# Two transformer blocks on one core: attention values with V as the weight, staged gelu, and two pieces of work in another order

## The chip, the core and the metric
One core of a Trainium2 chip. The kernel is one launch; its time is device microseconds, the median of the runs shown. All data are f32 in memory.

## What is computed
The reference runs two transformer blocks on x (512 tokens, width 1024), batch 1.

Block 1: RMS norm; a projection to q, k, v of 8 heads of 64, to gelu inputs u and vg (512 columns each) and a forget gate per head; causal attention with a cumulated log-forget bias; beside it a spatial gate over chunks of 128 tokens, u times (w_s applied to the normalised gelu(vg), plus a bias); `h = x + concat(att, sg) @ w_out`; an FFN of width 2816 with a causal depthwise convolution of 3 taps; a final RMS norm.

Block 2: an adaptive norm whose shift, scale and gates come from `silu(c) @ w_ada`; 8 heads of chunk attention ("ca", head size 64, normalised q and k, relative bias) and 8 heads of latent attention ("mla", 96 columns for q and k, rope on 32, 64 for v); an output projection, and an FFN of the same form.

```
p = softmax(logits)             # per head and 128 queries
out = einsum('bhqk,bkhd->bqhd', p, v)
uv = gelu(proj[..., V_END:G_END])
return rmsnorm(h, norm_final_g) # end of block 1
```

## The kernel before
Wide matrix products run as three float32r products each (high x high, high x low, low x high), so every weight piece is split: `load_split` (L337 to L353) reads a raw piece by a transfer on SP's queue, ScalarE casts it to the high part (L350), VectorE or GpSimd subtracts to get the low part (L351). `prefetch` keeps two pieces ahead (LOOK). There are 4 high and 4 low buffers.

TensorE's order is the program's own, written by hand; the other engines' order is made by a scheduler from the program's order and priorities. `high_priority` pulls work ahead, a negative offset pushes it behind, and `late()` (L528) orders an instruction behind the last one marked `urgent`. Two lists of generators, `Fill` objects, feed the attention loop: `fill` holds products (each yields its estimated ns), `bg` holds elementwise background work. `run(ns)` takes steps until the ns are used up, `upto(name)` takes all steps up to the end of a named job.

`attention` (L619 to L676) walks strips of 128 queries of one head. In step t it issues the scores of strip t (`strip_scores`, two or three products, a bias add with a running minimum on VectorE at L597, exp on ScalarE at L601), background work, half of the step's fill, the transposes of the exponentials of strip t-1 (`strip_turn`, L610, and their copy to pt at L612), the other half of the fill, and the values of strip t-2 (`strip_values`, L617): for each block of 128 keys a plain f32 product with P^T as the weight and 64 columns of V streaming, accumulated in the one `o` bank. Every 8 strips, that is two heads, `pair_end` (L709) takes the reciprocals of the 8 sums, scales `o` into `att` (L717), and one step later `turn` transposes att four times (L725) and splits the result into a high and a low part of `mix` (L741, L742). The last two heads run in half pairs of 4 strips. PSUM in attention has 4 `mm` banks, 3 `s` banks and 1 `o` bank. The p tiles, the gelu's and the norm's temporaries share one pool of 3 buffers (`pp`).

In block 1 the gelu is `gelu2` (L1108): two GpSimd instructions, a VectorE multiply (L1114), tanh on ScalarE (L1115) and a VectorE multiply into uv (L1116), on one token tile of 128x256 at a time. `gate(j)` (L1118) adds the squares on GpSimd and their sums on VectorE, `gelu_u(j)` (L1143) does the u columns; both are background work. The evacuation of q and k of a pair is at L1182 (qf) and L1186 (kf, marked urgent).

In block 2 `start` and `cq0` (L1473, L1489) compute the first projections; then `bg` gets the norm of cq0, the rope tables and `final`, block 1's final norm of x (L932 to L945: a scalar instruction, a pow on GpSimd, eight small products on TensorE and 16 VectorE multiplies at L942 into x in place). `ca_head` (L1615) transposes normalised q and k (L1633), then stacks them with copies (L686, L687, L696, L697) and a transfer of half a tile. `fill` goes through cq1, ck1, mla0, cv1, mla1 and the output products; `out0` first takes `bg` up to `final`, as it adds to x.

Of the kernel before, what the change touches and what calls it, by code (L numbers as in the profile page):

```python
# [19 lines left out]
P = 128  # L20
# [216 lines left out]
class Kernel:  # L237
# [367 lines left out]
    def strip_turn(self, hd, qi, sp):  # L605
        nk = (qi + 1) * P
        s, p = sp
        for kb in range(qi + 1):
            c = slice(kb * P, (kb + 1) * P)
            self.nc.tensor.transpose(s[:, c], p[:, c], self.ident)  # L610
        pt = self.pt.tile([P, 512], F32, tag="pt", name="pt")
        self.nc.any.tensor_copy(out=pt[:, :nk], in_=s[:, :nk])  # L612
        return pt

    def strip_values(self, hd, qi, pt, o):
        for kb in range(qi + 1):
            self.mm(o, pt[:, kb * P:(kb + 1) * P], hd["v"](kb), kb == 0, kb == qi)  # L617

    def attention(self, heads, fill, rate, bg, bgrate, mix, depth=1):  # L619
# [21 lines left out]
        for t in range(n + depth + 3):  # L641
            r = rate(t)
            if t < n:
                h, qi = seq[t]
                slices(h)
                sc[t] = self.strip_scores(hd[h], qi)
                for h in range(len(heads)):
                    if 0 < seq.index((h, 0)) - t <= LEAD:
                        slices(h, 1)
            with self.tc.high_priority(offset=-BEHIND):  # L650
                bg.run(bgrate(t))
            fill.run(r / 2)
            u = t - depth
            if 0 <= u < n:
                h, qi = seq[u]
                pt[u] = self.strip_turn(hd[h], qi, sc.pop(u))
            if t > n + depth:
                for f in later:
                    f()
                later = []  # L660
            fill.run(r / 2)
            for f in later:
                f()
            later = []
            u -= 1
            if 0 <= u < n:
                h, qi = seq[u]
                if u % 8 == 0:
                    o = self.bank("o")
                ov = 2 * qi + h % 2  # L670
                self.strip_values(hd[h], qi, pt.pop(u), o[:, ov * 64:(ov + 1) * 64])
                if h < last:
                    if u % 8 == 7:
                        later = [self.pair_end(o, mix, *hd[h]["end"])]
                elif u % 4 == 3:
                    later = [self.pair_end(o, mix, *hd[h]["end"], half=u % 8 // 4)]  # L676
# [32 lines left out]
    def pair_end(self, o, mix, sums, at, pool, tag, half=None):  # L709
# [4 lines left out]
        c8, c512 = slice(2 * qs[0], 2 * qs[-1] + 2), slice(qs[0] * P, (qs[-1] + 1) * P)  # L714
        nc.vector.reciprocal(sums[:, c8], sums[:, c8])
        att = self.att.tile([P, 512], F32, tag="att", name="att")
        nc.vector.tensor_tensor(out=att[:, c512].rearrange("p (g d) -> p g d", d=64),  # L717
                                in0=o[:, c512].rearrange("p (g d) -> p g d", d=64),
                                in1=sums[:, c8].unsqueeze(2).to_broadcast([P, 2 * len(qs), 64]),
                                op=ALU.mult)  # L720

        def turn():
            tp = self.bank("s")
            for t in qs:
                nc.tensor.transpose(tp[:, t * P:(t + 1) * P], att[:, t * P:(t + 1) * P], self.ident)  # L725
            if not half:
                t = pool.tile([P, 2, 512], F32R, tag=tag, name="mix")
                mix[at] = t[:, 0], t[:, 1]
            ins = self.split(mix[at], tp, c512)
            if half:  # L730

                self.before = ins
            mix[at, half] = True
# [299 lines left out]
    def block1_mix(self, xn, x, evac, evac_last, norm_a):  # L1033
        nc, i = self.nc, self.i
        ctx = self.c_mix = ExitStack()
        self.pt = self.pool("pt", 3, ctx=ctx)
# [50 lines left out]
        sqs = self.pt.tile([P, 512], F32, tag="pt", name="sqs")  # L1087
# [20 lines left out]
        def gelu2(v):  # L1108

            t = self.pp.tile([P, 512], F32, tag="p", name="gelu")[:, :256]  # L1110
# [3 lines left out]
            nc.vector.tensor_tensor(out=t, in0=t, in1=v, op=ALU.mult)  # L1114
            nc.scalar.activation(out=t, in_=t, func=AF.Tanh, scale=float(np.sqrt(2 / np.pi)))  # L1115
            nc.vector.scalar_tensor_tensor(out=v, in0=t, scalar=1.0, in1=v, op0=ALU.add, op1=ALU.mult)  # L1116

        def gate(j):  # L1118

            vs = [uv[t][:, 512 + 256 * j:768 + 256 * j] for t in range(4)]  # L1120
            for t, v in enumerate(vs):
                gelu2(v)
                sq = self.pp.tile([P, 512], F32, tag="p", name="sqg")[:, :256]
                nc.gpsimd.tensor_tensor(out=sq, in0=v, in1=v, op=ALU.mult)
                nc.vector.tensor_reduce(out=ss[:, j, t], in_=sq.rearrange("p (g d) -> p g d", d=64),
                                        axis=AX.X, op=ALU.add)
                yield 1200
# [15 lines left out]
        def gelu_u(j):  # L1143
            for t in range(4):
                gelu2(uv[t][:, 256 * j:256 * j + 256])
                yield 700
# [214 lines left out]
    def block2_mix(self, xn, norm_b, final, evac, evac_last, norm_a):  # L1361
# [3 lines left out]
        self.pt = self.pool("pt2", 3, ctx=ctx)  # L1365
# [4 lines left out]
        stk = self.pool("stk2", 12, ctx=ctx)  # L1370
# [94 lines left out]
        def ca_job(w, z, j, **kw):  # L1465
# [4 lines left out]
            if z < 2 and kw.get("pairs") != ((0, 1),):  # L1470
                bg.add(w, ca_norm(z, j))

# [16 lines left out]
        def cq0():  # L1489
# [3 lines left out]
            bg.add("final", final)  # L1493
# [195 lines left out]
        heads = [ca_head(h) for h in range(8)] + [mla_head(h) for h in range(8)]  # L1689
        self.attention(  # L1690
# [36 lines left out]
```

## Time and profile before
| | us |
|---|---|
| median of 3 runs | 1229.65 (1225.97 to 1230.58) |
| profiled execution, its own time | 1225.62 |
| span of that execution | 1223.9 |

The span runs from the first to the last instruction. PE is TensorE, PEld its weight loads, DVE VectorE, ACT ScalarE, POOL GpSimd. A TensorE record is longer than the spacing of records, since consecutive products overlap in the pipeline; the cost of one in a stream is the difference of two starts. A plain f32 product leaves two records, one for each of its passes. In brackets stand the idle time ahead of an instruction and what ended it.

### The profile page before, as it was taken

To read this page: it belongs to the slowest core of one execution; us is meant where nothing else is said; L and a number is where in the kernel's file an instruction comes from. 1 tells how busy PE (TensorE), PEld (TensorE's weight loads), DVE (VectorE), ACT (ScalarE), POOL (GpSimd) and SP (SyncE) were. 2 spreads that over 40 slices of the span, in tenths; PEclk is the share of its full clock that TensorE was granted. 3 is DMA by queue.
4 is the path that set the end of the run, shared out by engine and by line. 5 is a ranking of instruction groups with operands and counts; after the bars stand their busy time and mean duration, and the time that the engine had idled before them with its cause. 6 is when DMAs were issued, how large, how long until landed. Compare 5 with 4: busy or idle time off the path is not lost.

```text
span 1223.9 us, 17406 instructions
## 1 busy us (share of the span) xinstructions
PE 1193.0 (97%) x6730; PEld 1038.9 (85%) x6730; DVE 780.2 (64%) x1392; ACT 526.5 (43%) x946; POOL 190.5 (16%) x209
## 2 busy tenths in 40 slices
PE   9999898999999999999998989999999999999998
PEld 6898688988888888888998988899988888888887
DVE  6646777688888887433575878876675665653221
ACT  6535445454444443323434556655544444442110
POOL 2367301300000000000245472301200000000000
PEclk9999999999999999999999999999999999999999
DMA  7432222166666666433121333111133323233330
GB/s 237 120 102 78 82 82 61 53 188 196 200 192 190 193 190 190 144 98 128 58 86 57 87 109 104 36 36 36 53 123 102 103 86 104 93 89 112 114 110 18
DMA packets 42594, 135.78 MB, mean 111 GB/s; under 512 B 5120, under 2 KB 6016, under 8 KB 42512
## 3 DMA queue, kind: packets, MB, share of 16 engines
q1 hardware_dynamic: 34096, 106.84, 28.3%
q10 hardware_dynamic: 8208, 27.27, 7.4%
q8 instruction: 52, 0.85, 0.3%
q0 software_dynamic: 208, 0.57, 0.2%
q14 instruction: 30, 0.25, 0.1%
HBM read 128.37 MB, written 2.10 MB: 107 GB/s over the span
## 4 chain that ended last, share of the span: by engine, by line
PE 84%; DVE 6%; POOL 4%; issue 2%; ACT 2%; DMA 1%; SPq 0%; ACTq 0%; DVEq 0%; POOLq 0%
PE mm L372 74%; PE s L372 4%; PE o L372 3%; PE s L610 2%; POOL wlo L351 1%; ACT whi L350 1%; DVE wlo L351 1%; DVE s L597 1%; DVE ca L1457 1%; DMA x<-in_xT_dram 1%; POOL gelu L1111 0%; PE mm L1667 0%; DVE nt L557 0%; ACT p L601 0%; PE s L725 0%
## 5 line engine op out<-in xcount | busy, mean ns | idle before, releaser
L351 DVE TENSOR_TENSOR wlo<-wraw,whi 128x1024 fp32r<-128x1024 f32 (+4 forms) x182 | 210.3, 1157 | 180.6 <-ACT whi L350 179.5
L372 PE MATMUL mm<-xnh,whi 128*128 128x512 f32 (+1 forms) x832 | 310.8, 374 | 5.6 <-DVE x L877 2.7
L350 ACT CAST whi<-wraw 128x1024 fp32r<-128x1024 f32 (+4 forms) x194 | 191.6, 991 | 277.8 <-PE mm L372 260.2
L372 PE MATMUL mm<-xnl,whi 128*128 128x512 f32 (+1 forms) x832 | 309.7, 372 | 0.0
L372 PE MATMUL mm<-xnh,wlo 128*128 128x512 f32 (+1 forms) x832 | 309.7, 372 | 0.0
L372 PEld LDWEIGHTS mm<-xnh,whi 128*128 128x128 f32 x832 | 156.2, 188 | 33.5 <-DVE x L877 2.9
L372 PEld LDWEIGHTS mm<-xnh,wlo 128*128 128x128 f32 x832 | 156.1, 188 | 27.6
L372 PEld LDWEIGHTS mm<-xnl,whi 128*128 128x128 f32 x832 | 156.2, 188 | 26.7
L372 PE MATMUL mm<-gh,whi 128*128 128x512 f32 (+1 forms) x384 | 141.3, 368 | 1.1 <-DVE x L967 0.6
L372 PE MATMUL mm<-gh,wlo 128*128 128x512 f32 (+1 forms) x384 | 141.1, 367 | 0.0
L372 PE MATMUL mm<-gl,whi 128*128 128x512 f32 (+1 forms) x384 | 141.0, 367 | 0.0
L759 DVE SCALAR_TENSOR_TENSOR cv<-mm,cols,cv 128x510 f32<-128x510 f32 (+1 forms) x176 | 130.3, 745 | 2.5 <-ACT cv L757 0.5
L372 PE MATMUL mm<-whi,xnh 128*128 128x256 f32 (+3 forms) x304 | 96.5, 318 | 1.1 <-ACT xnh L842 1.1
L372 PE MATMUL mm<-wlo,xnh 128*128 128x256 f32 (+3 forms) x304 | 93.6, 308 | 0.2 <-DVE wlo L351 0.2
L372 PE MATMUL mm<-whi,xnl 128*128 128x256 f32 (+3 forms) x304 | 93.6, 308 | 0.1
L372 PEld LDWEIGHTS mm<-gh,whi 128*128 128x128 f32 x384 | 72.1, 188 | 13.5 <-DVE x L967 0.8
L372 PEld LDWEIGHTS mm<-gh,wlo 128*128 128x128 f32 x384 | 72.1, 188 | 12.1
L372 PEld LDWEIGHTS mm<-gl,whi 128*128 128x128 f32 x384 | 72.1, 188 | 12.0
L601 ACT ACTIVATE p<-s,st 128x128 f32<-128x128 f32 (+1 forms) x96 | 50.7, 528 | 70.4 <-DVE st L597 64.6
L1028 DVE CUSTOM_DVE_ANT_0 wada<-wada,cs,cols 128x1024 f32<-128x1024 f32 x48 | 61.5, 1282 | 28.9 <-DMA wada<-in_w_ada_dram 28.8
L372 PE MATMUL mm<-mix,whi 128*128 128x256 f32 (+1 forms) x288 | 73.8, 344 | 2.6 <-DVE x L877 1.5
L757 ACT ACTIVATE cv<-mm,cols 128x512 f32<-128x512 f32 x88 | 67.6, 773 | 0.0
(296 smaller groups left out, 1793.2 us busy)
## 6 DMA issues: line engine op xcount, KB each, us to landing
wraw<-in_w_up_dram SPq DMA_DIRECT2D x88, 512.0 KB, 3.6
wada<-in_w_ada_dram ACTq DMA_DIRECT2D x48, 512.0 KB, 3.7
wraw<-in_w_down_dram SPq DMA_DIRECT2D x32, 512.0 KB, 3.6
wraw<-in_w_out_dram SPq DMA_DIRECT2D x16, 512.0 KB, 3.7
wraw<-in_w_down_dram SPq DMA_DIRECT2D x16, 384.0 KB, 3.2
wraw<-in_w_qk_dram SPq DMA_DIRECT2D x8, 512.0 KB, 4.2
wraw<-in_w_v_dram SPq DMA_DIRECT2D x8, 256.0 KB, 4.9
x<-in_xT_dram SPq DMA_DIRECT2D x8, 256.0 KB, 6.5
```

The costliest lines, as they stand in the source:

```text
L350: nc.scalar.copy(hi[:, :n], raw[:, :n])
L351: (nc.gpsimd if pool else nc.vector).tensor_tensor(out=lo[:, :n], in0=raw[:, :n], in1=hi[:, :n].bitcast(F32), op=ALU.subtract)
L372: self.nc.tensor.matmul(out, lhsT, rhs, start=start, stop=stop, **kw)
L597: self.urgent = nc.vector.tensor_tensor_reduce(out=s[:, cs], in0=s[:, cs], in1=b, scale=1.0, scalar=3e38 if j == 0 else st[:, j - 1:j], op ...
L601: nc.scalar.activation(out=p[:, :nk], in_=s[:, :nk], func=AF.Exp, bias=st[:, len(parts) - 1:len(parts)], scale=-1.0, accum_out=hd["sums"](qi))
L610: self.nc.tensor.transpose(s[:, c], p[:, c], self.ident)
L757: nc.scalar.activation(out=t, in_=ps, func=AF.Identity, scale=w[2], bias=self.col(cb, n))
L759: nc.vector.scalar_tensor_tensor(out=t[:, d:], in0=ps[:, :512 - d], scalar=w[2 - d], in1=t[:, d:], op0=ALU.mult, op1=ALU.add)
L1028: nc.vector.tensor_tensor_reduce(out=w, in0=w, in1=self.cs, scale=1.0, scalar=self.col("b_ada_2", n), op0=ALU.mult, op1=ALU.add, accum_out ...
L1457: nc.vector.tensor_tensor(out=v3, in0=v3, op=ALU.mult, in1=ss[:, j, z, t].unsqueeze(2).to_broadcast([P, 4, 64]))
```

## The change
- **Values.** `strip_values` goes; `pair_values` does two heads at once at the end of a pair (in half pairs for the last two heads). V (128 keys x 64) is the weight, P^T of up to 512 queries streams, head 0 writes partitions 0 to 63 of the `o` bank and head 1 partitions 64 to 127, alternating by key block. So pt holds all blocks of a head (128 x 5 x 384, 2 buffers instead of 3 of 128 x 512).
- **Reciprocals.** `o` is now transposed already, so the four transposes of `pair_end` turn the broadcast reciprocals instead: ScalarE broadcasts 8 columns to 512, TensorE transposes them, ScalarE copies them out of PSUM, VectorE multiplies `o` by them, and the split reads SBUF.
- **Order in `attention`.** The turn of a finished pair and the values stand between the first half of the fill and the transposes of the strip.
- **Gelu.** Two token tiles at a time, with a yield between stages and `late()` on the VectorE instructions.
- **Block 2.** `final` is added to `bg` behind the norm of ck1; three rounds of `fill.run(1500)` and `bg.run(800)` stand ahead of `attention`; the stack pool has 9 tiles instead of 12.

```diff
-    def strip_turn(self, hd, qi, sp):
+    def strip_turn(self, pt, qi, sp):
...
-        pt = self.pt.tile([P, 512], F32, tag="pt", name="pt")
-        self.nc.any.tensor_copy(out=pt[:, :nk], in_=s[:, :nk])
-        return pt
-
-    def strip_values(self, hd, qi, pt, o):
-        for kb in range(qi + 1):
-            self.mm(o, pt[:, kb * P:(kb + 1) * P], hd["v"](kb), kb == 0, kb == qi)
+        a, b = divmod(qi, 3)
+        self.nc.any.tensor_copy(out=pt[:, a:a + qi + 1, b * P:(b + 1) * P],
+                                in_=s[:, :nk].rearrange("p (k q) -> p k q", q=P))
+
+    def pair_values(self, hds, pts, o, half=None):
+
+        q0, q1 = (0, 4) if half is None else (2 * half, 2 * half + 2)
+        for kb in range(q1):
+            a = max(q0, kb)
+            for z, (hd, pt) in enumerate(zip(hds, pts)):
+                p = pt.rearrange("p a b -> p (a b)")[:, (3 * kb + a) * P:(3 * kb + q1) * P]
+                self.mm(o[HALF_P[z], a * P:q1 * P], hd["v"](kb), p, kb == 0, kb == q1 - 1)
...
-            if 0 <= u < n:
-                h, qi = seq[u]
-                pt[u] = self.strip_turn(hd[h], qi, sc.pop(u))
-            if t > n + depth:
-                for f in later:
-                    f()
-                later = []
-            fill.run(r / 2)
             for f in later:
                 f()
             later = []
-            u -= 1
+            u = t - depth
+            w = u - 1
+            if 0 <= w < n and w % 8 == 7 or n - 8 <= w < n and w % 4 == 3:
+                h = seq[w][0]
+                half = None if h < last else w % 8 // 4
+                if not half:
+                    o = self.bank("o")
+                self.pair_values([hd[h - 1], hd[h]], [pt[h - 1], pt[h]], o, half)
+                later = [self.pair_end(o, mix, *hd[h]["end"], half=half)]
             if 0 <= u < n:
                 h, qi = seq[u]
...
+                if qi == 0:
+                    pt[h] = self.pt.tile([P, 5, 384], F32, tag="pt", name="pt")
+                self.strip_turn(pt[h], qi, sc.pop(u))
+            fill.run(r / 2)
...
+        att = self.att.tile([P, 512], F32, tag="att", name="att")
         nc.vector.reciprocal(sums[:, c8], sums[:, c8])
...
+        nc.scalar.copy(att[:, c512].rearrange("p (g d) -> p g d", d=64),
+                       sums[:, c8].unsqueeze(2).to_broadcast([P, 2 * len(qs), 64]))
...
-            ins = self.split(mix[at], tp, c512)
+            nc.scalar.copy(att[:, c512], tp[:, c512])
+            nc.vector.tensor_tensor(out=att[:, c512], in0=o[:, c512], in1=att[:, c512], op=ALU.mult)
+            ins = self.split(mix[at], att, c512)
...
-            t = self.pp.tile([P, 512], F32, tag="p", name="gelu")[:, :256]
+            t = self.pp.tile([P, 2, 256], F32, tag="p", name="gelu")
...
+            yield 800
+            with self.late():
+                nc.vector.tensor_tensor(out=t, in0=t, in1=v, op=ALU.mult)
             nc.scalar.activation(out=t, in_=t, func=AF.Tanh, scale=float(np.sqrt(2 / np.pi)))
...
+            yield 800
+            with self.late():
+                nc.vector.scalar_tensor_tensor(out=v, in0=t, scalar=1.0, in1=v, op0=ALU.add, op1=ALU.mult)
...
+            if w == "w_ck1":
+                bg.add("final", final)
...
-            bg.add("final", final)
...
+        for _ in range(3):
+            fill.run(1500)
+            bg.run(800)
         self.attention(
```

## Rows read from the trace of the kernel before

**Rows 1.** The page, part 1: TensorE's busy time, share, instructions.
```profile
PE 1193.0 (97%) x6730; PEld 1038.9 (85%) x6730; DVE 780.2 (64%) x1392; ACT 526.5 (43%) x946; POOL 190.5 (16%) x209
```

**Rows 2.** Busy time by stretch: length, then per engine us and count, clock, DMA.
```profile
55.00:215.00 160.00, 149.83 (x898) 129.52 (x897) 106.66 (x259) 73.97 (x165) 61.99 (x59) 1.00 0.28 82
654.50:665.00 10.50, 6.89 (x41) 6.12 (x40) 7.86 (x9) 4.86 (x6) 3.45 (x2) 0.84 0.25 63
665.00:840.00 175.00, 169.53 (x1283) 159.29 (x1284) 133.33 (x325) 101.91 (x262) 56.46 (x65) 1.00 0.23 66
```

**Rows 3.** TensorE in order of time, 654 to 665 us: start, length, instruction.
```profile
654.33 0.28 PE L372 MATMUL mm<-whi,xnl 128*128 128x256 f32 x1
...
658.45 1.21 PE L1633 MATMUL mm<-ident,ca 128*128 128x128 f32 x6 [2.17 <-DVE ca L1457]
...
659.67 0.42 PE L372 MATMUL mm<-wlo,xnh 128*128 128x256 f32 x1
...
664.90 0.36 PE L372 MATMUL s<-kl,qs 128*128 128x256 f32 x1 [0.20 <-DMA kl<-kl]
```

**Rows 4.** TensorE in order of time: three gaps in the two attention stages.
```profile
128.28 0.50 PE L372 MATMUL mm<-xnh,whi 128*128 128x512 f32 x1 [2.29 <-DVE kf L1186]
...
202.50 0.66 PE L610 MATMUL s<-ident,p 128*128 128x128 f32 x4 [0.72 <-ACT p L601]
...
708.79 0.63 PE L1633 MATMUL mm<-ident,ca 128*128 128x128 f32 x4 [2.66 <-DVE qs L687]
```

**Rows 5.** VectorE in order of time, ahead of two of these gaps.
```profile
127.20 0.42 DVE L1114 TENSOR_TENSOR gelu<-gelu,uv 128x256 f32<-128x256 f32 x1 [1.22 <-POOL gelu L1112]
127.54 0.68 DVE L1186 TENSOR_TENSOR kf<-mm,rrow 128x512 f32<-128x512 f32 x1
...
703.81 2.01 DVE L1457 TENSOR_TENSOR ca<-ca,ssc 128x256 f32<-128x256 f32 x4
```

**Rows 6.** Groups by line and shape, TensorE: one of three alike (vv, vc, vm).
```profile
L372 PE MATMUL o<-vc,pt 128*128 128x64 f32 x160 | 21.4, 264 | 0.4 <-ACT pt L612 0.4
```

**Rows 7.** TensorE in order of time, 683 to 688 us: two strips' values.
```profile
683.97 1.00 PE L372 MATMUL o<-vc,pt 128*128 128x64 f32 x8
684.77 0.42 PE L372 MATMUL s<-kh,qs 128*128 128x384 f32 x1
685.03 0.34 PE L372 MATMUL s<-kl,qs 128*128 128x384 f32 x1
685.21 0.28 PE L372 MATMUL mm<-whi,xnh 128*128 128x256 f32 x1
...
687.52 0.33 PE L372 MATMUL o<-vc,pt 128*128 128x64 f32 x2
687.66 0.48 PE L372 MATMUL s<-kh,qs 128*128 128x512 f32 x1
```

**Rows 8.** TensorE in order of time: 64-column weights (55 us), plain f32 (145 us).
```profile
55.15 0.22 PE L372 MATMUL mm<-tri,lfh 128*64 128x128 f32 x1
...
55.27 0.45 PE L372 MATMUL mm<-xnh,whi 128*128 128x512 f32 x1
55.55 0.39 PE L372 MATMUL mm<-xnl,whi 128*128 128x512 f32 x1
55.78 0.40 PE L372 MATMUL mm<-xnh,wlo 128*128 128x512 f32 x1
...
145.24 1.03 PE L372 MATMUL mm<-uv,wsp 128*128 128x256 f32 x4
```

**Rows 9.** Two tiles' instructions: count, ns shortest, median and longest, starts, forms.
```profile
L372 PE MATMUL mm<-uv,wsp x16: 377/379/483, 123.5 to 149.9; 128*128 128x256 f32 x16
...
L372 PEld LDWEIGHTS mm<-tri,lfh x4: 134/134/135, 53.9 to 55.0; 128*64 128x64 f32 x4
```

**Rows 10.** Groups by line and shape, ScalarE: the 512-wide copy out of PSUM.
```profile
L612 ACT COPY pt<-s 128x512 f32<-128x512 f32 x20 | 11.7, 584 | 8.1 <-PE s L610 7.8
```

**Rows 11.** Groups by line and shape, VectorE: the final norm's multiplies.
```profile
L942 DVE SCALAR_TENSOR_TENSOR x<-x,cols,mm 128x256 f32<-128x256 f32 x16 | 6.8, 473 | 0.2
```

More of the change, by code (lines that the diff above doesn't have):

```diff
@@ L664, in attention @@
             later = []
-            u -= 1
+            u = t - depth
[7 more added lines that the diff above has]
+                later = [self.pair_end(o, mix, *hd[h]["end"], half=half)]
             if 0 <= u < n:
                 h, qi = seq[u]
[L668 to L676, printed above, removed]
+                if qi == 0:
+                    pt[h] = self.pt.tile([P, 5, 384], F32, tag="pt", name="pt")
+                self.strip_turn(pt[h], qi, sc.pop(u))
+            fill.run(r / 2)
     def stacked(self, pool):
@@ L714, in pair_end @@
         c8, c512 = slice(2 * qs[0], 2 * qs[-1] + 2), slice(qs[0] * P, (qs[-1] + 1) * P)
+        att = self.att.tile([P, 512], F32, tag="att", name="att")
         nc.vector.reciprocal(sums[:, c8], sums[:, c8])
[L716 to L720, printed above, removed]
+        nc.scalar.copy(att[:, c512].rearrange("p (g d) -> p g d", d=64),
+                       sums[:, c8].unsqueeze(2).to_broadcast([P, 2 * len(qs), 64]))
         def turn():
@@ L1035, in block1_mix @@
         ctx = self.c_mix = ExitStack()
-        self.pt = self.pool("pt", 3, ctx=ctx)
+        self.pt = self.pool("pt", 2, ctx=ctx)
         self.pp = self.pool("pp", 3, ctx=ctx)
@@ L1084, in copy_to @@
             return lambda t, ps: scaled(dst(t), ps, t)
-        sqs = self.pt.tile([P, 512], F32, tag="pt", name="sqs")
+        sqs = self.pt.tile([P, 5, 384], F32, tag="pt", name="sqs").rearrange("p a b -> p (a b)")[:, :512]
         nc.scalar.activation(out=sqs, in_=x[0], func=AF.Square)
@@ L1113, in gelu2 @@
                                     op1=ALU.add)
-            nc.vector.tensor_tensor(out=t, in0=t, in1=v, op=ALU.mult)
+            yield 800
+            with self.late():
+                nc.vector.tensor_tensor(out=t, in0=t, in1=v, op=ALU.mult)
             nc.scalar.activation(out=t, in_=t, func=AF.Tanh, scale=float(np.sqrt(2 / np.pi)))
-            nc.vector.scalar_tensor_tensor(out=v, in0=t, scalar=1.0, in1=v, op0=ALU.add, op1=ALU.mult)
+            yield 800
+            with self.late():
+                nc.vector.scalar_tensor_tensor(out=v, in0=t, scalar=1.0, in1=v, op0=ALU.add, op1=ALU.mult)
         def gate(j):
             vs = [uv[t][:, 512 + 256 * j:768 + 256 * j] for t in range(4)]
-            for t, v in enumerate(vs):
-                gelu2(v)
-                sq = self.pp.tile([P, 512], F32, tag="p", name="sqg")[:, :256]
+            for a in (0, 2):
+                v = uvs[:, a:a + 2, 512 + 256 * j:768 + 256 * j]
+                yield from gelu2(v)
+                sq = self.pp.tile([P, 2, 256], F32, tag="p", name="sqg")
                 nc.gpsimd.tensor_tensor(out=sq, in0=v, in1=v, op=ALU.mult)
-                nc.vector.tensor_reduce(out=ss[:, j, t], in_=sq.rearrange("p (g d) -> p g d", d=64),
-                                        axis=AX.X, op=ALU.add)
-                yield 1200
+                yield 800
+                with self.late():
+                    nc.vector.tensor_reduce(out=ss[:, j, a:a + 2],
+                                            in_=sq.rearrange("p t (g d) -> p t g d", d=64),
+                                            axis=AX.X, op=ALU.add)
             nc.vector.tensor_scalar(out=ss[:, j], in0=ss[:, j], scalar1=1.0 / 64, scalar2=4 * EPS,
@@ L1143, in gelu_u @@
         def gelu_u(j):
-            for t in range(4):
-                gelu2(uv[t][:, 256 * j:256 * j + 256])
-                yield 700
+            for a in (0, 2):
+                yield from gelu2(uvs[:, a:a + 2, 256 * j:256 * j + 256])
+                yield 500
         def spatial(j):
@@ L1364, in block2_mix @@
         ctx = ExitStack()
-        self.pt = self.pool("pt2", 3, ctx=ctx)
+        self.pt = self.pool("pt2", 2, ctx=ctx)
         self.pp = self.pool("pp2", 3, ctx=ctx)
@@ L1369, in block2_mix @@
         two = self.pool("two2", 2, ctx=ctx)
-        stk = self.pool("stk2", 12, ctx=ctx)
+        stk = self.pool("stk2", 9, ctx=ctx)
         tabq, tabk = tabs = [one.tile([P, 4, 4, 16], F32, name="tab" + z) for z in "qk"]
```

1 line of the change is left out of this document (removed).

## Prediction
> **What bounds the kernel now.** I read the page's shares first: TensorE is busy 97% of the span [rows 1]. So time leaves this kernel either as TensorE work or as a TensorE gap. Next the table of stretches: the two attention stages, 55 to 215 us and 665 to 840 us, are 335 us long; TensorE is busy 149.8 of 160 and 169.5 of 175 there, VectorE 67% and 76% [rows 2]. TensorE's granted clock is full in both, so its work is worth its face value as long as the other engines keep pace. Third, TensorE in order of time around the start of the second attention: the first chunk head's transposes wait for the normalised q and k. The products ahead end near 654.45; the last six transposes start at 658.45, after 2.17 us idle with one wait before it, and the record of a 256-wide product, 0.28 us before, is then 0.42 us long [rows 3]: over these 10.5 us the mean granted clock is 0.84 [rows 2], so a part of them ran at 1.2 instead of 2.4 GHz. Last I read two other gaps of over 2 us that the change can touch, 2.29 us behind kf and 2.66 us behind qs [rows 4], and VectorE's order ahead of them [rows 5].
>
> **The change, part by part**
>
> **A. Products ahead of the first chunk head.** Three calls of 1500 ns (each k step is booked as 658 ns) take 7 steps of six 256-wide products, 42 x 0.117 = 4.9 us (0.117 is half of the 0.23 between 512-wide starts [rows 8]). They stand where TensorE now waits from 654.45 to 658.45. The last transposes would start near 659.4 instead of 658.45, 0.9 us later. The chain behind them (copies on ScalarE and VectorE, then the transfer of kl's halves) ends at the kl product, now at 664.90, then at 665.8. 4.9 - 0.9 = **4.0 us gained**. The lower clock disappears, but the shorter cover behind the transposes (5 steps at full speed, 3.5 us against a chain of 6.4 us) leaves about 2 us of new gap before the kl product; that is in the 4.0. Bounds: 3 us if q and k come later because VectorE also serves the new products' copies, 5.5 us if the chain tightens.
>
> **B. Values.** Now: one head is 10 products of 64 columns, each in two passes, 20 instructions with P^T as weights, 160 records for each of three groups of 8 heads [rows 6]. Eight take 683.97 to 684.77 = 0.80 us, two 0.14 us [rows 7]; by that slope (0.11 us each) the strips of 4 and 6 take 0.36 and 0.58: 1.88 us a head. After each strip's values the first score product costs 0.26 us where the next costs 0.18 [rows 7]: 0.08 a strip, 8 strips a pair. A pair now: 2 x 1.88 + 8 x 0.08 = **4.40 us**.
> After: per head V is the weight, and 512 + 384 + 256 + 128 = 1280 columns stream in two passes. The plain f32 product of 256 columns costs (1.03 - 0.38) / 3 = 0.217 us a pass [rows 8, 9]. One after the other a pair takes 2 x 1280 x 2 x 0.217 / 256 = 4.34 us. If the halves of the array run side by side, with starts in program order and each half busy with its own last pass, head 1's first pass runs beside head 0's second and so on; stepping through the 16 passes (0.43, 0.33, 0.22, 0.11 us) ends at **2.6 us**. No row shows two halves at once; the bounds are 2.6 and 4.34, and I take 2.6, since the program lists the halves alternately and the outputs share no partition. The price of changing to 64-column weights and back has a near row: two products with 64-column weights take 0.12 us (55.15 to 55.27), and the first full one after them 0.28 where 0.23 is usual (its 0.45 us record, too, is 0.06 longer) [rows 8], 0.05 us a change, 0.1 a pair. The values are now followed by transposes, so the 0.08 goes. A pair saves 4.40 - 2.7 = 1.7 us; 12 pairs, 20.4 us of TensorE.
> "TensorEngine Tiling" (Key Properties) of the Trainium skill says that a change of tiling mode drains the engine; a full drain, estimated as a product's record of 0.39 us less its spacing of 0.23, would be 0.16 us a change and 3.8 us in all, against 1.2 by the row; the sum below would be 2 to 3 us smaller.
> How much of 20.4 becomes time: VectorE rises to near 85% in the second stage, and with a strip's values gone from between scores and transposes, the exp chain has less cover. In the last pair of block 1 there are no products left, so nothing is gained there (1.7). I take 70% of 20.4, **14 us**; bounds 9 and 20.
>
> **C. Pair end and pt.** 12 pairs gain two 512-wide ScalarE copies (a broadcast of the reciprocals and one out of PSUM), 0.58 us each by the pt copy [rows 10]: 14 us of ScalarE in 335. In mid-stage the next strips' products hide them; without that cover each pair would pay 1.2 us. At the last half of each block they lie on the path: about 0.5 us twice, **+1**. The strided pt copy moves the same elements; 2 pt buffers and 9 stack tiles cost nothing as long as the tiles they replace were last read by a strip already on TensorE, which program order gives; a late one would hold a head's stacking, and its scores.
>
> **D. Gelu.** kf's evacuation starts at 127.54 behind a gelu multiply that itself waited 1.22 us for GpSimd; TensorE then waits 2.29 us for the bank [rows 4, 5]. Stages with a yield between, issued after the urgent instruction, put kf first; wide tiles halve the instructions. **-2.0**, bounds -2.3 and +1.5: the staged tile now holds one of 3 p buffers over up to two iterations, and an exp that draws it next waits, with its transposes behind it. The wait is queued on VectorE, where bias adds and bank copies come behind; the tanh and the spatial product's evacuation wait for it.
>
> **E. Final norm.** 16 VectorE multiplies of 0.47 us [rows 11], one scalar op, one pow on GpSimd, and its row products on TensorE pass behind the norms of cq1 and ck1 (two pows on GpSimd). So q and k of the third pair come some 7 us of VectorE earlier; their scaling (2.01 us from 703.81) lies right in front of the qs that TensorE waits for, 2.66 us [rows 4, 5]. **-1.5**, bounds -2.7 and +2, for the norm now holds one of four mm banks when the MLA products need two at a time.
>
> Sum: -4.0 - 14 + 1 - 2.0 - 1.5 = **-20.5 us** on the profiled execution of 1225.6 (span 1223.9), so 1205. The median of the runs shown is 1229.65, 4.0 above that execution; on it the change gives 1209.
>
> **The rivals**
>
> *Halves one after the other (0.20).* B is worth 12 x (4.40 - 4.34 - 0.1), about nothing. For it: no product of this trace overlaps another beyond the tail of the one before [rows 7, 8]. Against: all of those use the whole array. Sum -6.5: 1223.
>
> *Freed time turns into waits (0.08).* Block 1's last strips already wait for exp (0.72 us at 202.50 [rows 4]) where no products are left, and VectorE would be the bound. B is worth 3 us, sum -9.5: 1220. Against: in the second stage TensorE is idle 5.5 of 175 us with VectorE at 76% [rows 2].
>
> *Weight loads come into the open (0.10), slower.* Place: the 12 value blocks. With the halves serial and each of the 16 loads waiting for the running product, a load of up to 0.134 us (the 64-column record [rows 9]) adds 2.1 us a pair: 6.5 against 4.40, 12 x 2.1 = +25, with the rest +18.7: 1248. It decides from a block of 4.9 us on, where A, D and E are used up (6.5 / 12 = 0.5), and is measurable as slower from 5.4. Against: products with 64-column weights stand 0.06 us apart, loads included [rows 8].
> "TensorE: Matmul & The Clock Gate" (Part 3) of the Trainium skill states the rule behind this: a load overlaps running products only where row groups differ, and both halves use all rows. The trace does not bear it out so far: one row group throughout, yet no open loads.
>
> **How the numbers follow.** The forecast has 0.62: its own range is 1199 (A 5.5, B 20, C nothing, D 2.3, E 2.7) to 1215 (B 9). Serial halves 0.20, waits 0.08, open loads 0.10. The range 1199 to 1226 takes in the serial case with E's bad end, and leaves out the open loads and tails. About 0.5%, 6.1 us, is what a measurement of this kernel can tell from no change. Faster by more: most of 0.62, half of the serial case, most of 0.08: 0.74. Slower: 0.10. The rest, 0.16, is the same.
>
> **What would show it.** Right: value records of 64-column weights whose starts in a pair overlap, a block near 2.6 us between the products around it; no idle over 1 us ahead of the first chunk head and a granted clock of 1.00 there; a short gap at its kl product; no wait on kf; the final multiplies after 690. Wrong: blocks over 4.3 us; loads standing between value products; long waits of transposes on exp, or of score strips on p buffers; products waiting for a bank held by the final norm.

## The result and the profile after

The changed kernel takes 1238.37 us (median of 4, 1236.97 to 1239.08) against 1229.33 us for the kernel before beside it: ratio 1.0075, 95% interval 1.006 to 1.009. It is 9 us slower; the forecast was 20 us faster. The profiled execution took 1236.97 us, its span is 1235.3 us, its mean granted clock 0.989 (before: 0.997).

Page of the kernel after, part 1, as in [rows 1]:

```profile
PE 1184.5 (96%) x6458; PEld 1007.0 (82%) x6458; DVE 787.8 (64%) x1391; ACT 532.6 (43%) x947; POOL 187.5 (15%) x189
```

Its stretches, columns as in [rows 2], and four short ones behind 760 us:

```profile
55.00:215.00 160.00, 144.94 (x821) 118.82 (x820) 109.05 (x251) 78.91 (x167) 61.19 (x45) 1.00 0.28 80
654.50:665.00 10.50, 10.50 (x93) 10.50 (x92) 8.38 (x10) 3.66 (x6) 6.68 (x5) 1.00 0.08 25
665.00:840.00 175.00, 152.03 (x988) 125.37 (x989) 133.19 (x326) 99.91 (x251) 55.24 (x63) 0.95 0.24 68
...
760.00:764.00 4.00, 0.00 (x0) 0.00 (x0) 2.51 (x6) 1.11 (x5) 2.78 (x2) 0.81 0.08 32
764.00:768.00 4.00, 0.66 (x2) 0.23 (x2) 0.00 (x0) 0.00 (x0) 3.92 (x5) 0.50 0.00 0
768.00:772.00 4.00, 3.16 (x11) 2.27 (x11) 1.81 (x5) 1.22 (x3) 1.04 (x2) 0.50 0.00 0
772.00:776.00 4.00, 3.65 (x15) 3.30 (x16) 3.21 (x8) 2.08 (x7) 0.83 (x1) 0.50 0.00 0
```

TensorE has less to do: busy time by mean clock is 1184.5 x 0.989 = 1171.5 us of full-speed work, where before it was 1193.0 x 0.997 = 1189.4. But it is idle for 1235.3 - 1184.5 = 50.8 us, before 30.9. In block 1's attention it is busy 144.9 of 160 us (before 149.8), in block 2's 152.0 of 175 (before 169.5). The stretch ahead of the first chunk head, where TensorE was idle for a third of the time before, is full.

Where the 11 us of the span arise is told by the first product of each block's second FFN matrix (column "first to last start" of the operand gh; the kernel before, then after):

```profile
L372 PE MATMUL mm<-gh,whi x186: 279/389/389, 471.7 to 591.2; 128*128 128x512 f32 x154, 128*128 128x256 f32 x32
...
L372 PE MATMUL mm<-gh,whi x198: 279/389/390, 1099.2 to 1220.0; 128*128 128x512 f32 x154, 128*128 128x256 f32 x44
```

```profile
L372 PE MATMUL mm<-gh,whi x186: 279/389/389, 471.9 to 591.4; 128*128 128x512 f32 x154, 128*128 128x256 f32 x32
...
L372 PE MATMUL mm<-gh,whi x198: 279/389/389, 1110.6 to 1231.3; 128*128 128x512 f32 x154, 128*128 128x256 f32 x44
```

Up to block 1's mark both are level (471.7 and 471.9); from there to block 2's mark it is 627.5 us before and 638.7 after. I call the first the block 1 mark and the second the block 2 length below. The waits of TensorE there (640 to 870 us: who waits for whom, total, times, longest) and the largest of them in TensorE's order:

```profile
PE mm L1677 <- POOL mqk L1590: 8.9, 3, 7.2
PE s L611 <- ACT p L601: 6.6, 8, 2.0
PE mm L372 <- DVE mqk L1531: 1.8, 1, 1.8
PE s L372 <- ACT att L728: 1.8, 3, 0.7
```

```profile
759.27 0.28 PE L372 MATMUL s<-kl,qs 128*128 128x256 f32 x1
766.70 0.66 PE L1677 MATMUL mm<-ident,mqk 128*96 128x128 f32 x2 [7.15 <-POOL mqk L1590]
768.27 0.66 PE L1677 MATMUL mm<-ident,mqk 128*96 128x128 f32 x2 [0.91 <-POOL mqk L1590]
```

These are the first latent head's k transposes. They wait for the k norm of the latent heads (`k_norm`, the job mk0 of the list `bg`), whose pow and first multiplication run on GpSimd here, after and then before:

```profile
762.04 2.91 POOL L526 TENSOR_TENSOR nw<-nw,nhalf 128x16 f32<-128x16 f32 x1
765.03 1.04 POOL L1588 TENSOR_TENSOR mqk<-mqk,nw 128x512 f32<-128x512 f32 x1
```

```profile
728.52 2.91 POOL L526 TENSOR_TENSOR nw<-nw,nhalf 128x16 f32<-128x16 f32 x1 [0.95 <-DVE nw L1572]
731.51 1.04 POOL L1578 TENSOR_TENSOR mqk<-mqk,nw 128x512 f32<-128x512 f32 x1
```

It comes 33.5 us later than before. Following the two lists through the program step by step shows why. `bg` gets 1700 ns a step up to step 16 and 600 ns after; `run` drops what is left when the list is empty. With `final` no longer in it, `bg` is empty in steps 0, 1, 4, 5 and 6 and drops 0.4 + 1.7 + 0.4 + 1.7 + 1.7 = 5.9 us (before: 1.0 us once). Then `final` joins behind the norm of ck1 and ahead of kr, mq0 and mk0, and lasts into step 14. mk0 is left for the 600 ns steps; it is forced in step 27, when the first latent head asks for it. Before, it was done in step 23 without force.

### The profile page after: what moved, and what is told of

The parts are those of the page before. It is cut to its first block, busy times and chain, and to the rows that moved or that the text cites. A ratio compares the mean times of both kernels' runs of the same rounds, so it can differ in the third digit from the quotient of the medians.

```text
span 1235.3 us, 16818 instructions
## 1 busy us (share of the span) xinstructions
PE 1184.5 (96%) x6458; PEld 1007.0 (82%) x6458; DVE 787.8 (64%) x1391; ACT 532.6 (43%) x947; POOL 187.5 (15%) x189
## 4 chain that ended last, share of the span: by engine, by line
PE 82%; DVE 7%; POOL 4%; issue 3%; ACT 3%; DMA 1%; SPq 0%; ACTq 0%; POOLq 0%; DVEq 0%
PE mm L372 73%; PE s L372 4%; PE o L372 2%; PE s L611 2%; DVE s L597 1%; DVE wlo L351 1%; ACT p L601 1%; ACT whi L350 1%; DMA x<-in_xT_dram 1%; DVE x L955 0%; POOL nw L526 0%; DMA cs<-in_c_dram 0%; DVE nt L557 0%; DVE uv L1145 0%; POOL gelu L1113 0%
## 5 line engine op out<-in xcount | busy, mean ns | idle before, releaser
L372 PEld LDWEIGHTS mm<-gh,whi 128*128 128x128 f32 x384 | 72.0, 188 | 13.6 <-DVE x L968 0.8
```

The source lines that it names most:

```text
L372: self.nc.tensor.matmul(out, lhsT, rhs, start=start, stop=stop, **kw)
```

## The experiments

T1 to T4 are the explanations under test; each is told in brackets in the expectation where it first stands. All numbers in one table: median, ratio to the kernel before on the same chip with its 95% interval, and from the profiled execution TensorE's busy time, mean granted clock, idle time (span less busy) and the block 2 length. "-X" is the changed kernel with part X undone, "+X" the kernel before with X alone. All kernels but before, be and b0 have 9 stack tiles; no run takes the number of stack tiles by itself.

| kernel | us | ratio | busy | clock | idle | block 2 |
|---|---|---|---|---|---|---|
| before | 1228 to 1229 | 1 | 1193.0 | 0.997 | 30.9 | 627.5 |
| after | 1238.4 | 1.0075 (1.006 to 1.009) | 1184.5 | 0.989 | 50.8 | 638.7 |
| e1: -E | 1229.2 | 1.001 (0.9999 to 1.0021) | 1180.8 | 0.993 | 46.0 | 627.6 |
| e2: -A | 1241.0 | 1.0104 (1.0088 to 1.0119) | 1190.1 | 0.982 | 50.2 | 638.9 |
| e3: -B, -C | 1247.0 | 1.0171 (1.0147 to 1.0194) | 1203.4 | 0.986 | 41.6 | 647.9 |
| e4: -D | 1239.8 | 1.0095 (1.0079 to 1.011) | 1188.7 | 0.985 | 49.8 | 638.9 |
| b1: +B, +C | 1232.8 | 1.0033 (1.0017 to 1.0048) | 1185.4 | 0.987 | 44.9 | 631.5 |
| be: +E | 1238.3 | 1.0082 (1.0054 to 1.011) | 1200.0 | 0.990 | 36.7 | 637.9 |
| f1: `final` behind mk0 | 1234.1 | 1.0041 (1.0025 to 1.0057) | 1184.0 | 0.993 | 46.9 | 632.8 |
| f2: time of `bg` kept | 1235.6 | 1.0055 (1.0034 to 1.0076) | 1181.1 | 0.992 | 48.7 | 633.1 |
| g1: -E, even products | 1230.0 | 1.001 (0.9995 to 1.0024) | 1187.5 | 0.986 | 43.0 | 628.9 |
| ad: +A, +D | 1233.4 | 1.0044 (1.0027 to 1.0061) | 1196.3 | 0.996 | 31.7 | 627.8 |
| h0: -E, turn in mm | 1224.3 | 0.9963 (0.9949 to 0.9977) | 1178.8 | 0.994 | 41.8 | 628.0 |
| h2: h0, two strips deep | 1258.9 | 1.0244 (1.0226 to 1.0263) | 1195.8 | 0.986 | 61.0 | 656.8 |
| k1: after, busy in the wait | 1238.8 | 1.0093 (1.0076 to 1.011) | 1191.8 | 0.990 | 44.8 | 638.7 |
| p1: h0, bias and exp first | 1222.5 | 0.9956 (0.9939 to 0.9973) | 1180.6 | 0.993 | 39.8 | 625.6 |
| s1: h0, halves in turn | 1234.0 | 1.0056 (1.0044 to 1.0069) | 1192.4 | 0.994 | 39.9 | 635.0 |
| ha: h0, -A | 1228.9 | 1.0009 (0.9996 to 1.0023) | 1182.9 | 0.988 | 45.9 | 632.8 |
| hd: h0, -D | 1225.4 | 0.9976 (0.9964 to 0.9988) | 1176.2 | 0.997 | 44.2 | 624.2 |
| b0: before, turn in mm | 1224.8 | 0.9968 (0.9957 to 0.998) | 1196.4 | 0.994 | 26.8 | 627.1 |

A block's length in one profile carries the clock of that execution. h0 and hd have the same program in block 2 and almost the same waits there, yet 628.0 and 624.2 us: from 590 to 910 us the clock of hd is 1.00 throughout, that of h0 0.83 to 0.95 in four stretches of 10 us. The kernel after and e2 have the same block 1, and its mark stands at 471.9 and 476.7 us (clock in 55 to 215 us 1.00 and 0.96). So a difference of under some 4 us between two such lengths says little by itself.

### One part undone at a time

E undone (e1):

```diff
-            if w == "w_ck1":
-                bg.add("final", final)
...
+            bg.add("final", final)
```

> The changed kernel with part E alone undone: block 1's final norm joins the background list right after cq0, as in the kernel before. T1 (late k norm: the final norm behind ck1 stands ahead of the latent heads' norms in the background list, and TensorE waits for the k norm mk0 near 767 us and then runs at a low clock): the hole near 767 and the low clock behind it are gone, 1225 to 1229, 10 to 13 us below the changed kernel. T2 (the products ahead of the first chunk head are spent too early, so that later waits have no cover): a hole of the same size stays or moves, 1236 to 1240. T3 (the value blocks and the longer pair end make the waits): 1235 to 1240.

1229.2 us: the hole is gone and so is the whole loss, 9.2 us (T1 had said 10 to 13). T1 holds, T2 and T3 fall. But A to D together then stand level with the kernel before, though they were to bring 19. TensorE's work is 1180.8 x 0.993 = 1172.5 us, 17 less than before, and its idle time 15 more. Its waits in 640 to 870 us:

```profile
PE s L611 <- ACT p L601: 10.5, 11, 2.7
PE s L372 <- ACT att L728: 2.4, 4, 0.8
...
PE s L372 <- DMA kh<-kh: 1.4, 1, 1.4
...
PE s L372 <- DMA kl<-kl: 1.0, 1, 1.0
```

In the kernel before, the transposes waited 1.5 us for exp there, and nothing waited for a ScalarE copy behind the turn:

```profile
PE s L610 <- ACT p L601: 1.5, 2, 1.3
```

A undone (e2):

```diff
-        for _ in range(3):
-            fill.run(1500)
-            bg.run(800)
```

> The changed kernel with part A alone undone: no three rounds of products and background work ahead of the attention of block 2. T1: the hole at the latent heads' k norm stays (8 us of waits on it, clock low for some 10 us), the gap before the first chunk head's transposes comes back, 1240 to 1244. T2: the hole is gone or under 2 us, 1228 to 1234. T3: 1240 to 1244 too, with waits on exp as before.

B and C undone (e3), `strip_values`, `strip_turn`, `pair_end` and the three pt buffers of the kernel before:

```diff
-                self.pair_values([hd[h - 1], hd[h]], [pt[h - 1], pt[h]], o, half)
...
+                self.strip_values(hd[h], qi, pt.pop(u), o[:, ov * 64:(ov + 1) * 64])
```

> The changed kernel with parts B and C undone: P transposed as the weight, one strip's values at a time, three small pt buffers, reciprocals as in the kernel before. T1: the hole at the latent heads' k norm stays and what the values saved is lost, 1240 to 1250. T3 (value blocks and pair end are what costs): the waits on exp and on the turn's bank fall back to those of the kernel before and the time to 1224 to 1230. T2: 1238 to 1246 with the hole.

D undone (e4), the gelu on one token tile:

```diff
-            for a in (0, 2):
-                yield from gelu2(uvs[:, a:a + 2, 256 * j:256 * j + 256])
-                yield 500
+            for t in range(4):
+                gelu2(uv[t][:, 256 * j:256 * j + 256])
+                yield 700
```

> The changed kernel with part D alone undone: gelu on one token tile at a time, without stages. T1: only block 1's attention changes; the wait on kf comes back (2 us) and the waits of score strips on the turn's bank may fall (up to 3 us); 1237 to 1241, the hole in block 2 unchanged. T2 and T3 say the same, so this run prices D alone: if the staged gelu, not the pair end, lengthened block 1's waits, 1234 to 1236.

All three fell where T1 put them; in e2 and e4 T3 had said the same. Undoing A costs 2.6 us by the medians, undoing B and C 8.6, undoing D 1.4 (the intervals of after and e4 overlap, those of after and e2 touch). That the 2.6 are A's is not shown: A changes block 2 alone, whose length is the same in both profiles (638.7 and 638.9), while e2's block 1 mark is 4.8 us later.

### One part alone

B and C alone (b1: the diff of e3 read backwards, on the kernel before, with 9 stack tiles) and E alone (be: that of e1 read backwards):

> The kernel before with parts B and C alone: values on both halves, reciprocals turned instead of the values. T4 (the TensorE time that the values free turns into waits of the transposes on exp, whose chain of bias add on VectorE and exp on ScalarE had the strip's values as cover): TensorE busy 12 to 15 us less than before, idle as much more, 1226 to 1231. The prediction's own step B (70% of what is freed becomes time): 1213 to 1219.

> The kernel before with part E alone: block 1's final norm joins the background list behind the norm of ck1. T1: the list runs dry in the first 10 steps, the k norm mk0 is forced at the first latent head, TensorE waits 8 to 12 us on it and runs at a low clock behind it: 1242 to 1250. The prediction's step E (gain 2.7 to loss 2): 1226 to 1231.

Page of b1, part 1, and its largest waits in 640 to 870 us:

```profile
PE 1185.4 (96%) x6458; PEld 1009.5 (82%) x6458; DVE 782.1 (64%) x1402; ACT 536.0 (44%) x964; POOL 192.6 (16%) x209
```

```profile
PE s L611 <- ACT p L601: 7.3, 9, 2.3
PE mm L1634 <- DVE qs L687: 5.1, 2, 4.4
PE mm L1634 <- DVE ca L1458: 3.5, 2, 2.3
```

b1 is 4.4 us slower than the kernel before, a little past T4's range. Work fell from 1189.4 to 1185.4 x 0.987 = 1170.0 us, **19.4 us**. Idle time grew by 14.0 us, and the lower clock took 0.013 x 1185.4 - 0.003 x 1193.0 = 11.8 us of busy time. -19.4 + 14.0 + 11.8 = +6.4, by which the spans differ. So what the values save is there, and by this count all of it is given back, about half as waits and half as clock. The clock is no accident of this profile: the 12 executions of b1 have 0.987 to 0.990, those of the kernel before 0.990 to 0.997. Of the 14.0 us the waits on exp are 5.9 (9.5 us over the whole span, before 3.6); the others are spread over several banks and tiles (qs, kf, mqk, mix, att). E alone costs 9.9 us, less than the 14 to 22 that I had worked out from e3, but with the same wait (its longest on mk0 is 6.5 us).

### What of E costs

f1 moves `final` behind mk0; f2 leaves E's order, but `bg` keeps the time that it gets while empty:

```diff
             bg.add(f"mk{c}", k_norm(c))
+            if c == 0:
+                bg.add("final", final)
```

```diff
             if not t or t < 0:
-                self.debt = 0.0
+                self.debt *= self.keep
```

> The changed kernel with one difference: the final norm joins the background list behind the latent heads' k norm mk0, not behind the norm of ck1. T1 (what costs is the final norm's place ahead of kr, mq0 and mk0 in the list): no wait on the k norm, 1223 to 1229. If the cost is that the final norm runs in these steps at all (VectorE time taken at 700 to 716 us), the time stays at 1234 to 1239. T4 says that even so it does not go under 1222.

> The changed kernel with its order of jobs (final norm behind the norm of ck1), but the background list of block 2 keeps the time that it was given while it was empty. T1 in its narrow form (the loss is that the list is empty in the first 7 steps and its time is dropped): the k norm mk0 is then issued in step 20, not forced in step 27; the wait of 7 us on it goes, 1228 to 1233. If the final norm's 7.6 us of VectorE among the strips is what costs, as the run with it behind mk0 suggests: 1233 to 1236.

Counted as above, mk0 is now done in step 18 (f1) and 21 (f2), and no wait for it is left in either. Yet f1 is 4.9 and f2 6.4 us over e1; both fell in the case of the final norm's own time among the strips, not in T1's. So the wait at mk0 is worth only 3 to 4 of E's 9 us. f1 shows these waits in 640 to 870 us, which e1 has not:

```profile
PE mm L372 <- DVE mqk L1529: 1.8, 1, 1.8
PE mm L372 <- DVE x L943: 1.7, 2, 1.1
...
PE mm L372 <- ACT vm L1607: 1.2, 1, 1.2
```

4.7 us: banks that VectorE and ScalarE empty late, one of them the norm's own mm bank. My reading is that the final norm's 7.5 us of VectorE (16 x 0.47 [rows 11]) do this, as they now lie among the strips (739.0 to 747.1 us); in the kernel before they ran at 674 to 686 us, where the list held little else. But e1 has waits that f1 has not, and TensorE's idle time in the two profiles differs by 0.9 us only (46.9 and 46.0), its busy time by 3.2. What the other 5 to 6 us of E are stays open.

### Why the freed time is not kept

g1 hands the products out evenly, to keep some for the later strips:

```diff
-            lambda t: 3000 if t < 0 else 2000 if t < 16 else 1600 if t < 34 else 500,
+            lambda t: 3000 if t < 0 else 1500 if t < 34 else 500,
```

> The changed kernel with E undone and the products of block 2 handed out evenly: 1500 ns a step up to step 34 in place of 2000 up to step 16 and 1600 after. Counted from the two lists, the last products that need no finished head are then spent in step 30, not in step 25. T4 (strips without products beside them wait for exp): waits on exp between 655 and 840 us fall from 10.5 us to under 6, 1221 to 1226. If VectorE itself is the bound there, 1228 to 1231, as with E undone alone.

Waits on exp fell to 6.2 us, but others came (ca 2.8, qs 1.9, x 2.1) and the clock fell: 1230.0 us, no gain, and T4's 1221 to 1226 missed.

h0 takes the turn's bank from the mm banks, h2 lets two strips lie between scores and transposes, and p1 moves each strip's bias add and exp forward, all with E undone:

```diff
-            tp = self.bank("s")
+            tp = self.bank()
```

```diff
-    def attention(self, heads, fill, rate, bg, bgrate, mix, depth=1):
+    def attention(self, heads, fill, rate, bg, bgrate, mix, depth=2):
```

```diff
+        with self.tc.high_priority(offset=AHEAD):
             for j, (cs, b) in enumerate(parts):
```

> The changed kernel with E undone, and the turn of a pair takes its bank from the four mm banks, not from the three s banks that the score strips use. T4: the waits of score strips on the ScalarE copy behind the turn (5.5 us in E undone alone) go, the waits on exp stay at about 13 us; 1225 to 1228. If the mm banks are then what products wait for: 1229 to 1232.

> As the turn-in-mm kernel, and the exponentials of a strip are transposed two steps after its scores, not one (depth 2; four p buffers, for which pt is cut to the 13 blocks in use). T4 (the transposes wait since the chain through VectorE's bias add and ScalarE's exp is longer than one strip's products): waits on exp fall from 13 us to under 4, the granted clock stays nearer 1.00, 1215 to 1221, and both kernels are beaten. If VectorE's or ScalarE's throughput is the bound, or the three s banks (each strip now holds one for two steps): 1228 or more, with waits of score products on the pt copy.

> The turn-in-mm kernel (E undone) with each strip's bias add and exp scheduled ahead of other VectorE and ScalarE work by the priority that the first head's slices have; TensorE's order is the same. T4 with the queue as its cause: waits on exp fall from 15 us to under 8, 1217 to 1222. If the chain's own length is the cause, or the work that is pushed back is waited for instead: 1223 to 1228.

h0 gains 4.9 us on e1 and beats the kernel before; the waits behind the turn are gone and those on exp stay (14.9 us over the whole span), as T4 said; the time is a little under its range. h0's idle time is 10.9 us above that of the kernel before, and its waits on exp are 11.3 us longer. h2, which T4 put at 1215 to 1221, is 35 us slower than h0: transposes no longer wait for exp, but the scores wait for the three s banks, which each strip now holds for two steps. Its waits in 640 to 870 us:

```profile
PE s L372 <- ACT pt L612: 16.8, 24, 3.1
PE s L372 <- DVE pt L612: 7.4, 13, 2.1
```

p1 brings the waits on exp to 12.3 us over the span, not to under 8; its time is 1.8 us below h0's, not to be told apart. So the place in the queues is a small part of the wait. That the rest is the chain's length (scores, bias add, exp, transposes, copy, with three banks for it) is argued: no run shortens the chain.

ha and hd take A and D from h0 (diffs of e2 and e4), ad puts both on the kernel before:

> The turn-in-mm kernel with A undone. If A is worth what the changed kernel showed (2.6 us), 1226 to 1229; if it is worth nothing, as block 2's length in the kernel with A and D alone says, 1223 to 1226.

> The turn-in-mm kernel with D undone. If D is worth what the changed kernel showed: 1225 to 1227. If the staged gelu holds up exp (a strip's exp sat 4.6 us behind the gelu's last GpSimd instruction in the changed kernel) by as much as it frees kf: 1222.5 to 1225.

> The kernel before with parts A and D alone (products ahead of the first chunk head, staged gelu; 9 stack tiles). The prediction's steps A and D: 4 and 2 us, 1222 to 1224. From the runs so far (B and C alone 4.4 us over the kernel before, A to D together 0.9 over): A and D are worth 3.5 us, 1224 to 1226. If A only moves a wait to where the products are then missing: 1227 to 1230.

In h0 A is worth 4.7 us and D 1.2 (for D the intervals overlap). On the kernel before, A and D cost 5 us, which none of my cases held. In ad's profile the waits on ca and qs, 6.4 us in the kernel before, are gone, but others came in block 2: 2.5 us for `sq` L496 where the attention ends, 2.5 for kh and kl, 1.2 for the att that is to be turned. Its length is level with the kernel before (627.8 and 627.5), so no gain of A shows there. The block 1 mark is 3.8 us later (475.5), with 2.3 us of waits for the att that is to be turned; of these 3.8, be shows 2.4 as well (474.1), and its block 1 is that of the kernel before. Why just these waits come is open.

So the parts do not add up. B and C lose 4.4 us alone (b1), but gain 4.2 beside A and D (ad against e1) and 8.6 beside A, D and E (e3 against after). A and D lose 5.2 alone and gain 3.6 beside B and C (b1 against e1). E loses 9.9 alone, 9.2 beside all others and 13.6 beside A and D (ad against e3): of these three groups E's sign alone is the same in every company.

b0 is the control: the turn's bank in the kernel before.

> The kernel before with one edit: the turn of a pair takes its bank from the four mm banks. There its transposes wait 0.8 us in all and no score strip waits behind them, so it stays within 2 us of the kernel before: 1226 to 1230. If the bank alone is the gain: 1222 to 1225.

A miss: the bank alone gains 3.5 us. In TensorE's order at the start of block 1's FFN, before and b0:

```profile
230.35 0.39 PE L372 MATMUL mm<-xnh,whi 128*128 128x256 f32 x1 [2.72 <-DVE x L877]
```

```profile
230.01 0.38 PE L372 MATMUL mm<-xnh,whi 128*128 128x256 f32 x1 [0.58 <-DVE x L877]
```

2.1 us of it are here. That the turn shifts which mm bank is emptied last when the stage ends is my reading; no run isolates it. With it, h0 against b0 says what A to D are worth: 0.5 us, nothing that can be measured. h0, p1 and b0 all beat both kernels; b0 does so with one word.

### The two halves, and the clock behind a wait

s1 runs the value products of h0 head by head; k1 fills the wait on mk0 in the changed kernel with 28 products whose results are not used:

```diff
-        for kb in range(q1):
-            a = max(q0, kb)
-            for z, (hd, pt) in enumerate(zip(hds, pts)):
+        for z, (hd, pt) in enumerate(zip(hds, pts)):
+            for kb in range(q1):
+                a = max(q0, kb)
```

```diff
                 b = self.bank()
+                if h == 0 and scale is not None:
+                    for t in range(28):
+                        self.mm(b[:, :P], self.ident, self.ident, True, True)
```

> The turn-in-mm kernel with the same value products, head 0's all ahead of head 1's, so that neighbours in TensorE's order use the same half of the array. If the halves run at once only when the program alternates them, a pair's block takes 4.3 us in place of 2.4, TensorE is busy 15 to 20 us longer in total, and the time is between 1229 and 1242 (the cover makes up for a part). If the alternation does not matter, 1223 to 1226.

> The changed kernel with 28 plain products of 128 columns (identity by identity, into the bank that is overwritten next, some 6 us; their result is not used) ahead of the first latent head's k transposes, where TensorE waits 7.2 us for the k norm. The wait's end is set by GpSimd and stays where it is. If the low clock behind the wait (about 0.50 from 766 to 776 us) is a cost of its own, the clock there is near 1.00 and the time 1232 to 1235; if the wait alone costs, 1237 to 1240.

A pair's value block in TensorE's order, with what follows it, after and then s1:

```profile
753.43 2.37 PE L372 MATMUL o<-pt,vc 128*64 128x512 f32 x16
755.73 0.33 PE L611 MATMUL s<-ident,p 128*128 128x128 f32 x1
```

```profile
806.24 3.93 PE L372 MATMUL o<-pt,vm 128*64 128x512 f32 x16
810.10 0.33 PE L611 MATMUL s<-ident,p 128*128 128x128 f32 x1
```

The next instruction starts 2.30 us behind the block's start when the halves alternate, 3.86 when they do not; one product after the other, at the plain f32 rate of [rows 8, 9], would take 4.34. In the kernel after, blocks at full clock take 2.30 to 3.34 us. The long ones hold a wait of a weight load for the last strip's copy to pt, five times ScalarE's, 0.9 us at most:

```profile
PEld o L372 <- ACT pt L613: 2.6, 5, 0.9
```

TensorE is busy 13.6 us longer in s1 (12 x 1.56 would be 18.7) and the time is 9.8 us longer.

Three stretches of k1:

```profile
764.00:768.00 4.00, 3.29 (x30) 3.10 (x28) 0.02 (x1) 0.00 (x0) 3.92 (x3) 1.00 0.00 0
768.00:772.00 4.00, 2.30 (x13) 1.65 (x13) 1.26 (x2) 0.95 (x2) 2.54 (x4) 0.86 0.00 0
772.00:776.00 4.00, 3.15 (x14) 2.45 (x12) 3.04 (x10) 1.61 (x5) 0.83 (x1) 0.50 0.02 4
```

The clock holds through the wait and falls a few us later, behind short waits: 0.50 in 772 to 776 us as in the kernel after. The time is unchanged (1238.8 against 1238.4), in the range where the wait alone costs. But a good part of the low clock was only moved, so what it costs by itself is not settled by this run.

## Why the prediction was wrong

**E, the step that set the sign.** "So q and k of the third pair come some 7 us of VectorE earlier": the wait on qs did go, with E alone too (be has none). But it goes with A as well (e1 has none either), so the 1.5 us were no gain that E could add. And the step named what the final norm was moved behind, and not what it was moved ahead of: kr, mq0 and mk0 in the same list, with a lower rate from step 16 on and a head that forces mk0. Nor did it ask what fills the list where the norm had been. Bounds -2.7 to +2; measured +9.2 (after against e1) and +9.9 alone: 3 to 4 us of it the wait at mk0 (f1, f2), the rest open. The bound's reason, the norm's mm bank, shows in f1 (x L943, 1.7 us), not among the waits of the kernel after.

**B, the step that set the size.** The work was right: 20.4 us forecast, 19.4 measured (b1); a block 2.6 forecast, 2.30 measured where it waits for nothing. Serial halves and open loads are refuted by the same rows. "I take 70% of 20.4; bounds 9 and 20" failed, with C 13 us net: b1 is 4.4 us slower, so alone the share kept is none; beside A and D it is 4.2 us, and with E too 8.6. The rival "freed time turns into waits" named the place, with a chance of 0.08, and still priced it at 3 us gained. I weighed it by VectorE's 76% in [rows 2], a question of throughput; the near 85% forecast for the second stage did not come (133.19 of 175 us, 76%). The waits point to the time of one strip's chain instead: up to 2.7 us on exp with VectorE 64% busy over the span. And I counted no clock for waits, 11.8 us in b1.

**C.** +1 forecast. In the traces the two copies cost not as ScalarE time, but as a bank: one s bank is held from the turn's transposes to the copy L728. The copy sat behind an exp that waited for VectorE, in the kernel after (ScalarE, then TensorE):

```profile
114.57 0.58 ACT L601 ACTIVATE p<-s,st 128x384 f32<-128x384 f32 x1 [2.16 <-DVE st L597]
...
115.14 0.57 ACT L728 COPY att<-s 128x512 f32<-128x512 f32 x1
...
115.77 0.50 PE L372 MATMUL s<-kh,qs 128*128 128x512 f32 x1 [2.57 <-ACT att L728]
```

5.5 us of such waits in e1, none in h0. How much of h0's 4.9 us is this and how much the shift that b0 shows can't be separated.

**A.** Right in its mechanism: 1.00 in place of 0.84 ahead of the first chunk head, and two gaps of 1.35 and 1.02 us (kh, kl) for the 2 us forecast. The gaps of the kernel after:

```profile
667.23 0.36 PE L372 MATMUL s<-kh,qs 128*128 128x256 f32 x1 [1.35 <-DMA kh<-kh]
668.61 0.35 PE L372 MATMUL s<-kl,qs 128*128 128x256 f32 x1 [1.02 <-DMA kl<-kl]
```

-4.0 forecast, -4.7 measured beside B (ha; -2.6 by e2's median, which its block 2 length does not bear out), none without B (ad, by the block 2 length of one profile).

**D.** -2.0 forecast; the wait on kf is gone in the kernel after, and its undoing costs 1.2 to 1.4 us, within the measurement. That D gains is not shown.

**The sum.** It added five terms, each read from the kernel before. Without E the change is level with the kernel before (e1), where the other four were to bring 19 us: the same part has another sign in another company. The bounds' upper end, too, is 1214 by its own terms (1229.65 - 15.5), not 1215; nothing hangs on it.

## What to carry to other kernels

Freed time on the busiest engine is worth something only where no other chain ends just behind it: before counting it, look at how long one turn of the loop's chain takes without that work as cover, and how many banks it may hold meanwhile. When a job is moved in a list that is served by a budget, follow the whole list: what stands empty where it was, what stands behind it where it goes, and which of those has a date. Undo parts and add parts: here A is worth 4.7 us beside B and shows no gain without it, B and C lose 4.4 us alone and gain 4.2 beside A and D, and a one-word control on the kernel before (1224.8 us) comes as near to the best kernels with the change (1224.3 and 1222.5) as can be measured here.

## What the runs showed of the hardware that was not expected

- Two 64-column halves run at once when the program alternates them, 2.30 us for 16 records, and far less so when one half's products all come first, 3.86 us. "TensorEngine Tiling (Array Packing)" (Key Properties) of the Trainium skill says that different tiles can run in parallel; the runs agree, with that condition.
- The kernel before by itself: of 92 executions 21 had a mean granted clock of 0.997 and took 1225.3 to 1228.0 us, 35 had 0.994 (1227.2 to 1230.6), 11 had 0.991 (1230.5 to 1232.4). The wait at 230 us left the clock at 1.00 in 228 to 240 us in the profile of the kernel before (2.72 us) and at 0.86 in that of e1 (2.65 us). So one profile's clock is not the kernel's.
